# RWKV layer: one-operand feature steps and activation splits move from GpSimd to ScalarE

## The chip, the cores and the metric

The kernel runs on one core of a Trainium2 chip. The metric is the device time of one execution in microseconds (us), as the median of three runs. The engines are named as in the profile: PE is the TensorE matmul and PEld its weight load, DVE is VectorE, ACT is ScalarE, POOL is GpSimd, SP is SyncE, which here issues the DMAs. A name such as L1136 is a line of the kernel before.

## The reference, cut to what matters

The whole program is one gated-recurrence block followed by four layers (convolution, RWKV, attention, convolution) on 512 tokens and 256 context tokens with 1024 channels, in fp32. The change lies in the RWKV layer alone, in what is computed ahead of its recurrence:

```python
xx = centred_shift(h) - h
lerp = lambda n: h + xx * mu[n]
k = lerp(2) @ w_k
v = heads(lerp(3) @ w_v)
kk = heads(k * k_k); kk = kk * rsqrt(sum(kk * kk) + 1e-12)
xw, xa = lerp(1), lerp(4)
for d in range(2):
    w_log = -softplus(-(w0[d] + tanh(xw @ w1[d]) @ w2[d])) - 0.5
    dec = exp(-exp(w_log))
    a = sigmoid(a0[d] + (xa @ a1[d]) @ a2[d])
    dirs.append((heads(dec), heads(k * (1.0 + (a - 1.0) * k_a)), heads(a)))
r = heads(lerp(0) @ w_r)
g = lerp(5) @ w_g
```

The recurrence then runs over these features in both directions, and its output goes through a norm, a gate and a last projection.

## The kernel before

Matrix products keep fp32 precision by a split: an operand becomes a rounded high part (fp32r) and the low part that is left, and three matmuls stand for one product. For weights ScalarE makes the high part (`whi`, L172) and VectorE the low part (`wlo`, L175). For activations `split_x` has a switch: the high part is a copy on GpSimd (L274) or on ScalarE (L272), and the low part a subtraction on VectorE (L275). In the RWKV layer the switch stands at GpSimd everywhere.

The layer has these stages in program order. A matrix `h` of 128 partitions by 8 tiles of 770 columns (tokens and context, channels on partitions) is made. The k projection runs (`proj_fm`, 8 output blocks of 8 k-tiles each), with the low-rank products for decay and `a` fed in between; for its first lerp GpSimd also adds the two neighbours (L1017). The r projection runs next, and after each of its 8 output blocks `features(p)` is called. That makes two units (one for each half of the 768 tokens) of two directions, thus 32 passes of the loop body in `part2`. Then come the g projection (two halves), with the first preparations of the recurrence (`ahead`, whose scores are L1280) placed behind its first half, and the v projection. `part1` makes the two tanh tiles `tz` and `ta` (L1108) from small matmuls (L1105, L1106) in two PSUM banks. For a direction, `part2` then adds 1 to `tz` (L1120, GpSimd), scans it along the tokens (L1123, VectorE), takes two exponentials (L1126, L1127, ScalarE), copies six columns into `pcs` (L1128, GpSimd), and forms the halves of the tiles AR (L1132 VectorE, L1133 GpSimd) and F (L1139 GpSimd, L1141 VectorE) from `kd` (L1136 and L1137, GpSimd) and `ta` (L1140, VectorE, in place, so it waits until L1136 has read `ta`). F and AR go to DRAM by SyncE's queue (L1143) and are read back for the recurrence (L1254). `features` also splits two small weight tiles (`lwh`, L1165, GpSimd).

Each engine carries out its instructions in the order of its own queue. That order is set by a planner that simulates the program with its own costs; weight loads and their splits are given a higher priority. The buffers are few: two of F and AR each, three of `tz`, `ta` and `kd`, eight of `lhi` and `llo` each (the high and low parts of a lerp's eight tiles), two PSUM banks for the small matmuls.

Of the kernel before, what the change touches and what calls it, by code (L numbers as in the profile page):

```python
# [10 lines left out]
F32 = mybir.dt.float32  # L11
F32R = mybir.dt.float32r
AF = mybir.ActivationFunctionType
ALU = mybir.AluOpType
# [4 lines left out]
P = 128  # L19
# [10 lines left out]
FB=[int(c) for c in "2221122333"]  # L30
RB=2
LB=8
BA=[int(c) for c in "0100"]
NE=2
DQ=lambda nc,i: {"s":nc.sync,"a":nc.scalar,"p":nc.gpsimd}["ssss"[i]]
WB=3
# [34 lines left out]
class K:  # L71
# [860 lines left out]
    def rwkv_layer(self, X, XC):  # L932
        nc, ins, tc = self.nc, self.ins, self.tc
# [12 lines left out]
        WH = 770  # L946
# [8 lines left out]
        lp = self.pool(esl, "rwl", side="right")  # L955
        hp = self.pool(esl, "rwh", side="right")
        h = hp.tile([P, KT, WH + 2], F32, name="h")
# [30 lines left out]
        c1 = lp.tile([P, 8], F32, name="c1")  # L988
        c2 = lp.tile([P, 8], F32, name="c2")
        kkc = lp.tile([P, 8], F32, name="kkc")  # L990
        nc.vector.tensor_scalar(w0h, self.col("rwkv_w0_2", 0, 16), 0.5, None, ALU.mult)
        nc.vector.tensor_scalar(a0h, self.col("rwkv_a0_2", 0, 16), 0.5, None, ALU.mult)
        nc.vector.tensor_scalar(c2, self.col("rwkv_k_a_2", 0, 8), 0.5, None, ALU.mult)
# [3 lines left out]
        pcs = lp.tile([P, 2, NP, 12], F32, name="pcs")  # L997
# [9 lines left out]
        def lerp_k(n, k, hi, lo):  # L1007
            t = stg.tile([P, WH], F32, name="l32", bufs=LT)
            nc.vector.scalar_tensor_tensor(t, xx[:, k, :], self.col("rwkv_mu_2", 8 * n + k), h[:, k, 1:WH + 1],
                                           ALU.mult, ALU.add)  # L1010
            self.split_x(hi, lo, t, BA[2] and n in (0, 3, 5))

        def lerped(n, first=False):
            his, los = [], []
            for k in range(KT):
                if first:
                    nc.gpsimd.tensor_tensor(xx[:, k, :], h[:, k, 0:WH], h[:, k, 2:WH + 2], ALU.add)  # L1017
                    nc.vector.scalar_tensor_tensor(xx[:, k, :], xx[:, k, :], 0.5, h[:, k, 1:WH + 1], ALU.mult, ALU.subtract)
                his.append(lerp.tile([P, WH], F32R, name="lhi"))
                los.append(lerp.tile([P, WH], F32R, name="llo"))  # L1020
                lerp_k(n, k, his[k], los[k])
            return (lambda k: his[k]), (lambda k: los[k])
# [43 lines left out]
        def feat(name, i, shape=(P, 384)):  # L1066
            return fp.tile(list(shape), F32, name=name, bufs=FB[i])
# [23 lines left out]
        def part1(p, q, lw):  # L1091

            u = Ctx()
            u.p, u.q, u.n, u.qs = p, q, 2 * p + q, slice(q * 384, (q + 1) * 384)
            u.r, u.k, u.kkh = feat("r", 0), feat("k", 1), feat("kkh", 2)
            nc.sync.dma_start(u.k, k_d[p][:, u.qs])
            for hh in range(2):
                nc.sync.dma_start(u.kkh[hs[hh]], rn_d[2 * p + hh, u.qs].partition_broadcast(64))
            nc.sync.dma_start(u.r, r_d[p][:, u.qs])
            u.tz, u.ta = [], []  # L1100
            for i, x, bias, name, outs in ((0, t1, w0h, "tz", u.tz), (1, a1, a0h, "ta", u.ta)):
                pss = [self.ptr.tile([P, 512], F32, name="tr")[:, :384] for _ in range(2)]
                wh, wl = lw[i]
                for d in range(2):
                    nc.tensor.matmul(pss[d], wh[:, d, :], x[d][:, u.qs], start=True, stop=False)  # L1105
                    nc.tensor.matmul(pss[d], wl[:, d, :], x[d][hs[0], u.qs], start=False, stop=True)  # L1106
                    t = feat(name, 7 + i)
                    nc.scalar.activation(t, pss[d], AF.Tanh, scale=0.5, bias=bias[:, 8 * d + p:8 * d + p + 1])  # L1108
                    outs.append(t)
            return u  # L1110

        def part2(u):
            p, q = u.p, u.q

            nc.vector.scalar_tensor_tensor(u.kkh, u.k, kkc[:, p:p + 1], u.kkh, ALU.mult, ALU.mult)
            u.kds = []
            for d in range(2):

                tz, ta = u.tz[d], u.ta[d]
                (nc.vector if BA[3] == 1 else nc.gpsimd).tensor_scalar(tz, tz, 1.0, 1.0, ALU.mult, ALU.add)  # L1120
                rv = (lambda t: t) if d == 0 else (lambda t: t[:, 383::-1])
                od = (lambda t: t) if d == 0 else (lambda t: t[:, :, 63::-1])
                nc.vector.tensor_tensor_scan(rv(tz), rv(m64[:, d:384 + d]), rv(tz), 0.0, ALU.mult, ALU.add)  # L1123
                Ed = E[(d + 2 * u.n) % len(E)]
                Ein, Eex, en = Ed[:, :, 1 - d:65 - d], Ed[:, :, d:64 + d], 64 * (1 - d)
                nc.scalar.activation(Ein, c3(tz), AF.Exp, scale=-dh)  # L1126
                nc.scalar.activation(tz, tz, AF.Exp, scale=dh)  # L1127
                nc.gpsimd.tensor_scalar(pcs[:, d, p, 6 * q:6 * q + 6].unsqueeze(2), Ed[:, :, en:en + 1], 1.0, 1.0,  # L1128
                                        ALU.mult, ALU.mult)
                F, AR = [feat(nm, i, (P, WH))[:, :TA].rearrange("p (c f t) -> p c f t", f=2, t=64)  # L1130
                         for nm, i in (("F", 5), ("AR", 6))]
                nc.vector.scalar_tensor_tensor(od(AR[:, :, 0, :]), Eex, -2.0, c3(u.kkh), ALU.mult, ALU.mult)  # L1132
                nc.gpsimd.tensor_tensor(AR[:, :, 1, :], Ein, c3(u.r), ALU.mult)  # L1133
                kd = feat("kd", 9)
                (nc.scalar.activation(kd, ta, AF.Identity, scale=c2[:, p:p + 1], bias=c1[:, p:p + 1]) if BA[0]
                 else nc.gpsimd.tensor_scalar(kd, ta, c2[:, p:p + 1], c1[:, p:p + 1], ALU.mult, ALU.add))  # L1136
                (nc.gpsimd if BA[1] else nc.vector).tensor_tensor(kd, kd, u.k, ALU.mult)  # L1137
                u.kds.append(kd)
                nc.gpsimd.tensor_tensor(F[:, :, 1 - d, :], c3(kd), c3(tz), ALU.mult)  # L1139
                nc.vector.scalar_tensor_tensor(ta, ta, 1.0, u.kkh, ALU.add, ALU.mult)  # L1140
                nc.vector.tensor_tensor(od(F[:, :, d, :]), c3(ta), c3(tz), ALU.mult)  # L1141
                for t, dst_ in ((F, f_d[d]), (AR, ar_d[d])):
                    DQ(nc, 1).dma_start(dst_[6 * q:6 * q + 6, :, p].rearrange("c q f t -> q c (f t)"),  # L1143
                                      t.rearrange("q c f t -> q c (f t)"))

            u.bp = u.kds[0]
            nc.vector.tensor_tensor(u.bp, u.kds[0], u.kds[1], ALU.add)
            nc.vector.scalar_tensor_tensor(u.bp, u.r, self.col("rwkv_r_k_2", p), u.bp, ALU.mult, ALU.mult)

        def part3(u):  # L1150
            ps = self.ptr.tile([P, 512], F32, name="tr")
            for i in range(3):
                nc.tensor.matmul(ps[:, 2 * i:2 * i + 2], u.bp[:, i * P:(i + 1) * P], sel2, start=True, stop=True)
            nc.vector.tensor_scalar(bon[:, 3 * u.q:3 * u.q + 3, 2 * u.p:2 * u.p + 2],
                                    ps[:, :6].rearrange("p (i h) -> p i h", h=2), 0.5, None, ALU.mult)

        def features(p):
            lw = []
            for src in (w2, a2):
                wh = fp.tile([P, 2, P], F32R, name="lwh", bufs=2)  # L1160
                wl = fp.tile([64, 2, P], F32R, name="lwl", bufs=2)
                w32 = fp.tile([P, 2, P], F32, name="lw32")
                for hh in range(2):
                    nc.sync.dma_start(w32[hs[hh]], src[:, :, p * P:(p + 1) * P])
                nc.gpsimd.tensor_scalar(wh, w32, 1.0, 1.0, ALU.mult, ALU.mult)  # L1165
                nc.vector.tensor_tensor(wl, w32[hs[0]], wh[hs[0]].bitcast(F32), ALU.subtract)
                lw.append((wh, wl))
            for q in range(2):
                units.append(part1(p, q, lw))
                if len(units) > 2:  # L1170
                    part3(units[-3])
                if len(units) > 1:
                    part2(units[-2])

        def done_r(p, t):
            DQ(nc, 0).dma_start(r_d[p], t)
            features(p)
# [370 lines left out]

        vhi, vlo = [[lerp.tile([P, WH], F32R, name=n) for _ in range(KT)] for n in ("lhi", "llo")]
        for k in range(KT):  # L1550
            self.split_x(vhi[k], vlo[k], h[:, k, 1:WH + 1], BA[2])
        xh, xl = (lambda k: vhi[k]), (lambda k: vlo[k])
        for nh in range(2):
            lnb = bp.tile([P, 512], F32, name="lnb")
# [51 lines left out]
        with ExitStack() as es:  # L1606
            op = self.pool(es, "rwo")
            work = self.pool(es, "rwow", bufs=2)
            hi = op.tile([P, KT, TA], F32R, name="ry_hi")
            lo = op.tile([P, KT, TA], F32R, name="ry_lo")  # L1610
# [427 lines left out]
```

## Time and profile before

| what | value |
|---|---|
| median of 3 runs | 2716.43 us (2715.82 to 2716.82) |
| the profiled execution | 2723.18 us, its span 2721.5 us |
| mean granted TensorE clock over the span | 0.924 |

The busy time of an engine is a share of the whole span; stages differ, so the rows below are of the stretch from 814 us to 1345 us, in which the layer's `h` is finished, the projections and features are made, and the recurrence's first scores begin. A wait is the idle time of an engine ahead of an instruction, put down to what ended it. The granted clock is a share of the full 2.4 GHz, mean over a stretch.

### The profile page before, as it was taken

To read this page: it belongs to the slowest core of one execution; us is meant where nothing else is said; L and a number is where in the kernel's file an instruction comes from. 1 tells how busy PE (TensorE), PEld (TensorE's weight loads), DVE (VectorE), ACT (ScalarE), POOL (GpSimd) and SP (SyncE) were. 2 spreads that over 40 slices of the span, in tenths; PEclk is the share of its full clock that TensorE was granted. 3 is DMA by queue.
4 is the path that set the end of the run, shared out by engine and by line. 5 is a ranking of instruction groups with operands and counts; after the bars stand their busy time and mean duration, and the time that the engine had idled before them with its cause. 6 is when DMAs were issued, how large, how long until landed. Compare 5 with 4: busy or idle time off the path is not lost. (4 is left out here: it accounts for less than half of the span.)

```text
span 2721.5 us, 48392 instructions
## 1 busy us (share of the span) xinstructions
PE 2398.6 (88%) x19837; PEld 1900.8 (70%) x19867; DVE 1693.8 (62%) x2577; ACT 1014.6 (37%) x1861; POOL 714.7 (26%) x700
## 2 busy tenths in 40 slices
PE   6998869899896888898699886889999899997996
PEld 4776657777574766666588775768788788875655
DVE  4434356985457588888678874545255378548836
ACT  4642343111431233232355553233333366422223
POOL 0101001000205269888222541210000178300001
PEclk8998988899897989899599998889999999998998
DMA  5523542434322227655523443533455411222331
GB/s 151 147 85 101 155 140 70 118 90 118 91 85 63 76 93 225 182 183 170 186 96 132 145 141 103 201 106 98 132 155 153 137 43 43 68 93 78 86 95 55
DMA packets 352942, 319.06 MB, mean 117 GB/s; under 512 B 19679, under 2 KB 292032, under 8 KB 352208
## 3 DMA queue, kind: packets, MB, share of 16 engines
q1 hardware_dynamic: 352720, 315.95, 38.4%
q8 instruction: 157, 2.57, 0.4%
q14 instruction: 65, 0.53, 0.1%
HBM read 241.85 MB, written 64.63 MB: 113 GB/s over the span
## 5 line engine op out<-in xcount | busy, mean ns | idle before, releaser
L175 DVE TENSOR_TENSOR wlo<-wraw,whi 128x1024 fp32r<-128x1024 f32 x212 | 268.0, 1265 | 461.9 <-ACT whi L172 446.3
L172 ACT ACTIVATE whi<-wraw 128x1024 fp32r<-128x1024 f32 x212 | 224.2, 1058 | 732.7 <-PE mm L202 414.0
L202 PE MATMUL mm<-hT_lo,whi 128*128 128x512 f32 (+1 forms) x864 | 322.8, 374 | 0.0
L201 PE MATMUL mm<-hT_hi,whi 128*128 128x512 f32 (+1 forms) x864 | 318.4, 380 | 1.0 <-ACT h L680 1.0
L204 PE MATMUL mm<-hT_hi,wlo 128*128 128x512 f32 (+1 forms) x864 | 289.6, 371 | 0.5 <-DVE wlo L175 0.5
L807 DVE SCALAR_TENSOR_TENSOR cvo<-ypad,dwh,cvo 128x784 f32<-128x784 f32 (+1 forms) x270 | 236.4, 905 | 4.5
L204 PEld LDWEIGHTS mm<-hT_hi,wlo 128*128 128x128 f32 x864 | 163.6, 190 | 39.1 <-issue 1.4
L201 PEld LDWEIGHTS mm<-hT_hi,whi 128*128 128x128 f32 x864 | 164.6, 191 | 35.7 <-issue 13.0
L202 PEld LDWEIGHTS mm<-hT_lo,whi 128*128 128x128 f32 x864 | 164.6, 191 | 33.0 <-issue 6.3
L220 PE MATMUL mm<-whi,hT_hi 128*128 128x512 f32 x384 | 152.7, 399 | 1.3 <-ACT hT_hi L265 1.3
L221 PE MATMUL mm<-wlo,hT_hi 128*128 128x512 f32 x384 | 152.6, 397 | 0.0
L222 PE MATMUL mm<-whi,hT_lo 128*128 128x512 f32 x384 | 149.8, 399 | 0.0
L767 POOL MEMSET ypad<- 128x15 f32 x16 | 1.8, 114 | 500.2 <-DVE cvo L807 274.0
L201 PE MATMUL mm<-lhi,whi 128*128 128x256 f32 (+1 forms) x256 | 83.5, 369 | 16.8 <-POOL lhi L274 15.6
L202 PE MATMUL mm<-llo,whi 128*128 128x256 f32 (+1 forms) x256 | 89.3, 370 | 8.7 <-DVE llo L275 8.5
L220 PE MATMUL mm<-whi,lhi 128*128 128x512 f32 x192 | 82.7, 433 | 11.3 <-DVE so L1536 5.9
L220 PEld LDWEIGHTS mm<-whi,hT_hi 128*128 128x128 f32 x384 | 72.7, 189 | 19.0 <-issue 2.4
L221 PE MATMUL mm<-wlo,lhi 128*128 128x512 f32 x192 | 80.9, 421 | 5.7 <-DVE wlo L175 5.7
L585 PE MATMUL tr<-mraw,sc 128*32 128x128 f32 x1536 | 68.2, 295 | 18.1 <-DMA mraw<-in_mod_w_dram 14.0
L221 PEld LDWEIGHTS mm<-wlo,hT_hi 128*128 128x128 f32 x384 | 72.6, 189 | 15.6 <-issue 1.2
L222 PEld LDWEIGHTS mm<-whi,hT_lo 128*128 128x128 f32 x384 | 71.9, 189 | 15.9 <-issue 1.8
L1287 ACT ACTIVATE Df<-ps 32x128 f32<-32x128 f32 x176 | 68.1, 387 | 37.5 <-PE ps L1280 35.2
(502 smaller groups left out, 5897.0 us busy)
## 6 DMA issues: line engine op xcount, KB each, us to landing
mraw<-in_mod_w_dram SPq DMA_DIRECT2D x96, 512.0 KB
wraw<-in_conv_w_in_dram SPq DMA_DIRECT2D x48, 512.0 KB
wraw<-in_attn_w_in_dram SPq DMA_DIRECT2D x48, 512.0 KB
wraw<-in_w_in_dram SPq DMA_DIRECT2D x24, 512.0 KB
f_d<-F SPq DMA_DIRECT2D x32, 384.0 KB
ar_d<-AR SPq DMA_DIRECT2D x32, 384.0 KB
F<-f_d SPq DMA_DIRECT2D x24, 512.0 KB
AR<-ar_d SPq DMA_DIRECT2D x24, 512.0 KB
```

The costliest lines, as they stand in the source:

```text
L172: nc.scalar.activation(hi[:, :n], raw, AF.Copy)
L175: nc.vector.tensor_tensor(lo[:, :n], raw, hi[:, :n].bitcast(F32), ALU.subtract)
L201: nc.tensor.matmul(ps[s], wh[:, k, :], xh(k)[:, a:b], start=k == 0, stop=False)
L202: nc.tensor.matmul(ps[s], wh[:, k, :], xl(k)[:, a:b], start=False, stop=False)
L204: nc.tensor.matmul(ps[s], wl[:, k, :], xh(k)[:, a:b], start=False, stop=k == kts - 1)
L220: nc.tensor.matmul(ps, h, wh[:, kk, :], start=k == 0, stop=False)
L221: nc.tensor.matmul(ps, h, wl[:, kk, :], start=False, stop=False)
L222: nc.tensor.matmul(ps, l, wh[:, kk, :], start=False, stop=k == kts - 1)
L585: nc.tensor.matmul(ps[g:g + 32, 0:P], self.sc[:, k, :], raw[:, k, :], start=k < 4, stop=k >= 4)
L767: nc.gpsimd.memset(yp_[:, 0:15], 0.0)
L807: nc.vector.scalar_tensor_tensor(acc, yp_[:, tap:tap + W], dwh[:, tap, kt:kt + 1], acc, ALU.mult, ALU.add)
L1287: nc.scalar.activation(s.Df[rows, :, :, gsl].rearrange("p t a u -> p u a t"), p3[rows, :, 32 * b:32 * b + 32].rearrange("p u (a t) -> p u ...
```

## The change

Five steps move from GpSimd to ScalarE; what is computed stays the same. The activation splits of all lerps (of 770 columns: 24 into `lhi` and 16 low-rank ones into F) and of the 8 tiles for v make their high part on ScalarE. In `part2`, `tz + 1` becomes an activation with a bias operand (a new tile `one`, set once), `pcs` a copy, and `kd`'s first step an activation with a scale and a bias operand. In `features` the copy into `lwh` moves. The split of the squares in `done_k` (L1076) stays on GpSimd, as do the products with two tensor operands (L1133, L1137, L1139). The line of L1137 is only rewritten: it ran on GpSimd before as well.

```diff
+        one = lp.tile([P, 1], F32, name="one")
+        nc.vector.memset(one, 1.0)
...
-            self.split_x(hi, lo, t, BA[2] and n in (0, 3, 5))
+            self.split_x(hi, lo, t, True)
...
-                (nc.vector if BA[3] == 1 else nc.gpsimd).tensor_scalar(tz, tz, 1.0, 1.0, ALU.mult, ALU.add)
+                nc.scalar.activation(tz, tz, AF.Identity, bias=one)
...
-                nc.gpsimd.tensor_scalar(pcs[:, d, p, 6 * q:6 * q + 6].unsqueeze(2), Ed[:, :, en:en + 1], 1.0, 1.0,
-                                        ALU.mult, ALU.mult)
+                nc.scalar.activation(pcs[:, d, p, 6 * q:6 * q + 6].unsqueeze(2), Ed[:, :, en:en + 1], AF.Copy)
...
-                (nc.scalar.activation(kd, ta, AF.Identity, scale=c2[:, p:p + 1], bias=c1[:, p:p + 1]) if BA[0]
-                 else nc.gpsimd.tensor_scalar(kd, ta, c2[:, p:p + 1], c1[:, p:p + 1], ALU.mult, ALU.add))
-                (nc.gpsimd if BA[1] else nc.vector).tensor_tensor(kd, kd, u.k, ALU.mult)
+                nc.scalar.activation(kd, ta, AF.Identity, scale=c2[:, p:p + 1], bias=c1[:, p:p + 1])
+                nc.gpsimd.tensor_tensor(kd, kd, u.k, ALU.mult)
...
-                nc.gpsimd.tensor_scalar(wh, w32, 1.0, 1.0, ALU.mult, ALU.mult)
+                nc.scalar.activation(wh, w32, AF.Copy)
...
-            self.split_x(vhi[k], vlo[k], h[:, k, 1:WH + 1], BA[2])
+            self.split_x(vhi[k], vlo[k], h[:, k, 1:WH + 1], True)
```

## Rows read from the trace of the kernel before

**Rows 1.** The page, busy time of each engine over the span.

```profile
PE 2398.6 (88%) x19837; PEld 1900.8 (70%) x19867; DVE 1693.8 (62%) x2577; ACT 1014.6 (37%) x1861; POOL 714.7 (26%) x700
```

**Rows 2.** Stretches: us, busy us of PE, PEld, DVE, ACT, POOL; clock; DMA.

```profile
814.00:860.00 46.00, 21.86 (x78) 15.47 (x78) 38.76 (x32) 11.04 (x20) 30.07 (x23) 0.65 0.21 70
...
968.00:1120.00 152.00, 131.32 (x570) 98.47 (x568) 133.18 (x132) 46.18 (x87) 134.56 (x104) 0.90 0.52 159
1120.00:1200.00 80.00, 69.76 (x269) 50.06 (x269) 71.60 (x83) 28.32 (x51) 69.77 (x64) 0.94 0.64 197
1200.00:1295.00 95.00, 81.70 (x325) 60.61 (x323) 79.36 (x104) 29.09 (x52) 75.87 (x70) 0.91 0.59 183
1295.00:1345.00 50.00, 31.68 (x255) 27.51 (x256) 33.64 (x83) 17.37 (x41) 13.56 (x15) 0.55 0.61 199
```

**Rows 3.** PE's waits, 814 to 1295 us: total, times, longest.

```profile
PE mm L201 <- POOL lhi L274: 15.6, 3, 11.5
...
PE tr L1105 <- ACT ta L1108: 4.0, 3, 1.4
```

**Rows 4.** POOL's groups by line and shape, 815 to 1310 us.

```profile
L1136 POOL TENSOR_SCALAR kd<-ta,c,c 128x384 f32<-128x384 f32 x32 | 48.1, 1503 | 2.3 <-ACT ta L1108 1.3 <-POOL pcs L1128 0.9
L1133 POOL TENSOR_TENSOR AR<-E,r 128x384 f32<-128x384 f32 x32 | 45.6, 1427 | 12.7 <-DMA r<-r_d 12.7
...
L274 POOL TENSOR_SCALAR lhi<-l 128x770 fp32r<-128x770 f32 x24 | 35.4, 1478 | 7.6 <-DVE l L1009 6.6 <-DVE bon L1154 0.9
L1120 POOL TENSOR_SCALAR tz<-tz 128x384 f32<-128x384 f32 x32 | 31.8, 1000 | 1.0 <-ACT tz L1108 1.0
L1128 POOL TENSOR_SCALAR pcs<-E 128x6 f32<-128x6 f32 x32 | 20.1, 629 | 16.3 <-ACT E L1126 14.8 <-DMA kkh<-rn_d 1.5
...
L274 POOL TENSOR_SCALAR F<-l 128x770 fp32r<-128x770 f32 x16 | 15.8, 985 | 24.2 <-PE tr L1078 14.5 <-DVE l L1009 6.6 <-DVE t L1051 2.0
```

**Rows 5.** DVE's groups by line and shape, 815 to 1310 us.

```profile
L1123 DVE TENSOR_TENSOR_SCAN tz<-m,tz 128x384 f32<-128x384 f32 x32 | 38.3, 1208 | 2.6 <-POOL tz L1120 2.5
L1141 DVE TENSOR_TENSOR F<-ta,tz 128x384 f32<-128x384 f32 x32 | 32.9, 1028 | 1.3 <-ACT tz L1127 0.7
L1140 DVE SCALAR_TENSOR_TENSOR ta<-ta,kkh 128x384 f32<-128x384 f32 x32 | 27.9, 870 | 19.0 <-POOL kd L1136 19.0
```

**Rows 6.** Single lines: shortest, median and longest instruction in ns.

```profile
L1120 POOL TENSOR_SCALAR tz<-tz x32: 507/815/4348, 968.8 to 1275.3; 128x384 f32<-128x384 f32 x32
...
L1123 DVE TENSOR_TENSOR_SCAN tz<-m,tz x32: 920/956/1767, 976.6 to 1276.6; 128x384 f32<-128x384 f32 x32
...
L1141 DVE TENSOR_TENSOR F<-ta,tz x32: 541/1246/1641, 988.4 to 1287.3; 128x384 f32<-128x384 f32 x32
...
L1140 DVE SCALAR_TENSOR_TENSOR ta<-ta,kkh x32: 539/633/1645, 985.0 to 1286.0; 128x384 f32<-128x384 f32 x32
```

**Rows 7.** DVE's waits, 968 to 1295 us: total, times, longest.

```profile
DVE ta L1140 <- POOL kd L1136: 19.0, 21, 3.3
DVE lwl L1166 <- POOL lwh L1165: 5.2, 4, 2.5
```

**Rows 8.** ACT's waits, 968 to 1295 us: total, times, longest.

```profile
ACT E L1126 <- DVE tz L1123: 101.9, 25, 8.3
```

**Rows 9.** ACT's groups by line and shape, 815 to 1310 us.

```profile
L1108 ACT ACTIVATE tz<-tr,w0h 128x384 f32<-128x384 f32 x32 | 18.2, 580 | 41.7 <-DVE F L1141 22.3 <-PE tr L1106 10.5 <-POOL F L1139 5.4
...
L964 ACT ACTIVATE h<-mm,mod,gs 128x512 f32<-128x512 f32 x8 | 5.8, 797 | 0.0
...
L1050 ACT ACTIVATE t<-F 64x768 fp32r<-64x768 f32 x2 | 1.7, 843 | 0.2 <-POOL F L1048 0.2
L1108 ACT ACT_TABLE_LOAD x1 | 1.3, 1283 | 0.0
```

**Rows 10.** Timeline, SyncE: a late store of F, the first reading back.

```profile
1289.75 0.39 SPq L1143 DMA_DIRECT2D f_d<-F  x1
...
1294.18 0.44 SPq L1254 DMA_DIRECT2D F<-f_d  x1
```

More of the change, by code (lines that the diff above doesn't have):

```diff
@@ L32 @@
 LB=8
-BA=[int(c) for c in "0100"]
 NE=2
```

## Prediction

> **What bounds the kernel now.** I read the page first. PE is the busiest engine, POOL the least busy one [rows 1], so over the whole span nothing seems to be won by taking work from POOL. The share over the span misleads here: the table of stretches shows that POOL's work is bunched. From 968 to 1120 us POOL is busy 134.56 of 152 us (89%), DVE 133.18 (88%), PE 131.32 (86%) and ACT 46.18 (30%); the next two stretches look alike [rows 2]. Over these three, 327 us, ACT's share is 103.6 us (46.18 + 28.32 + 29.09), or 32%. Three engines are near full, each waits for the others, and the fourth has room.
>
> Which of the three sets the pace? I looked at waits next. PE's recorded waits for POOL's `lhi` are 15.6 us in three pieces, one of them 11.5 us, and those are all at the starts of projections [rows 3]. In the body of the features the wait that stands out is ACT's: 25 times, 101.9 us in all, an exponential waits for DVE's scan [rows 8]. ACT is thus not short of time, it is behind DVE. DVE in turn idles 19.0 us, 21 times, until L1136 on POOL has read `ta`, and 5.2 us until POOL has made `lwh` [rows 7]. And while DVE is busy, it is slow: L1141 takes 541 ns at its shortest and 1246 ns at the median, and POOL's L1120 goes from 507 ns to 4348 ns [rows 6]. Instructions of one shape that vary so much are held up by something else that runs; I read it as DVE and POOL getting in each other's way. So the pace of the features is DVE's, stretched and interrupted by POOL.
>
> The end of the stage counts too. A late F store is issued at 1289.75 us, the first reading back at 1294.18 us [rows 10], and from 1295 to 1345 us PE runs at a mean granted clock of 0.55 with 31.68 of 50 us busy [rows 2]: the scores have nothing to hide under, because features and projections end together. Features that end sooner than the projections would change that.
>
> **The change part by part.** I count on the profiled execution's own time, 2723.2 us (span 2721.5 and 1.7 around it); that is 6.8 us above the median of 2716.4, and the difference that I find is taken off the median.
>
> *What POOL loses.* L1136 48.1 us, L1120 31.8, L1128 20.1, the 24 `lhi` splits 35.4, the 16 F splits 15.8: 151.2 us [rows 4], and besides these 16 small `lwh` copies and the last 8 `lhi` splits, which I leave out of the sum. No DMA moves: the stores of F and AR stay in SyncE's queue and come when the features are done.
>
> *What ACT gains.* `tz + 1` is like the tanh of the same shape, 32 x 0.58 = 18.6 us; `kd` lies between that and the 512-column activation with scale and bias operands (0.797), I take 0.69, 32 x 0.69 = 22.1; `pcs` lies between nothing and 0.58, for six columns I take 0.3, 9.6; `lwh` at most 0.58, I take 0.5, 16 x 0.5 = 8.0; a split as the copy of 768 columns, 0.843 [rows 9], and 24 of them fall into the 327 us, 20.2. Together 78.5 us, so ACT goes from 103.6 to 182 us of 327 (56%). Some 24 more splits, 20.2 us, fall before 968 us, where ACT has 35 of 46 us free in the first stretch [rows 2].
>
> *814 to 860 us.* POOL gives up eight splits behind its eight neighbour sums, and PE's wait of 11.5 us is for one of these splits [rows 3]. DVE is busy 38.76 of 46 us here [rows 2] and makes three operations per tile itself, so it takes over as the limit soon. Bounds: nothing to 11.5 us. I take 5.
>
> *860 to 968 us.* The 16 low-rank F splits leave a POOL that is not full (15.8 us in 16 pieces, mean 985 ns, [rows 4]) for an ACT that has one of 843 ns [rows 9]. I take nothing; what hides it is the k projection's matmul stream. If a split there sticks behind a weight split that waits for a buffer, it costs some microseconds; that is in the bounds.
>
> *968 to 1295 us, DVE's waits.* `kd` now follows the tanh in ACT's own queue, so `ta` is read well before DVE comes to overwrite it: the 19.0 us go, and with `lwh` the 5.2: 24 us [rows 7].
>
> *968 to 1295 us, DVE's stretching.* The excess over the shortest is 32 x (1208 - 920) = 9.2 us for the scan, 32 x (1028 - 541) = 15.6 for L1141, 32 x (870 - 539) = 10.6 for L1140 [rows 5, 6]; 35.4 us for the three. How much goes with the moved operations? L1136, L1120 and L1128 make 100.0 us [rows 4] of POOL's 280.2 us (134.56 + 69.77 + 75.87) [rows 2], 36%. I take that share, 13 us. Bounds: nothing (the kept products fill the place) and 35.
>
> A rule of the Trainium skill speaks against this part (GPSIMD Engine Reference, section 4.1, Engine selection): it calls one-input operations on GpSimd roughly line rate and two-input ones about twice slower, so the change takes away what that engine does well and leaves what it does badly. The shortest L1120, 507 ns against 580 ns for the tanh of this shape on ACT [rows 6, 9], agrees. If that were all, the sum would be no gain at all, against my 13 and 24 us; it feeds the third rival.
>
> *What ACT's fuller queue costs.* The queue is in order. Behind an exponential that waits for the scan now stand more things that others need: `whi` splits, PSUM evictions, `lhi`. PE waited 4.0 us for ACT's `ta` [rows 3]. With ACT's work up by three quarters (182 over 103.6) I take 7 us as the price. Bounds: 3 and, worked out below, 66.
>
> *The sum.* -5 - 24 - 13 + 7 = -35 us. DVE is busy nearly nine tenths of the time, so I let it through to the end in full. PE could follow: over the 327 us it is busy 282.8 (131.32 + 69.76 + 81.70), at a clock of 0.90 to 0.94 [rows 2], so with fewer gaps and a fuller clock it needs well under 290. That gives 2688 us by the profiled execution, and 2716.4 - 35 = about 2681 us as the median.
>
> **The rivals.**
>
> *First, the recurrence's first scores slip under the projections.* If the planner lets the features end clearly before the v projection, the 50 us from 1295 to 1345 us, at clock 0.55 [rows 2], are partly covered by matmuls of v. For it: features are held by DVE and POOL, and both get lighter. Against: PE's queue spreads the small matmuls of the features evenly along g and v, and both end together now [rows 10]. If half of the 50 us is hidden, 2681 - 25 = 2656 us; if nearly all, 2635.
>
> *Second, slower: splits stuck in ACT's queue.* The mechanism is one: an `lhi` split for the r or g projection stands behind an exponential that waits for the scan, on average 101.9 / 25 = 4.1 us, at most 8.3 [rows 8], and PE, which cannot go on without that tile, stops, as it did when POOL was late [rows 3]. There are 16 such splits. All of them stuck cost 16 x 4.1 = 66 us: 2681 + 66 - 7 = 2740 us. It decides when the cost, instead of 7, reaches 42 + 5, that is with 12 stuck splits. For it: ACT's wait is frequent in just this stretch. Against: if DVE gets faster, that wait gets shorter, and the planner puts the splits of later tiles ahead.
>
> *Third, no change.* The kept products with two operands stand between the same neighbours (L1133 alone 45.6 us, two more like it, [rows 4]), and hold DVE up as long as before; the waits of rows 7 become waits for L1137, which still follows `kd` on POOL. Then only the first 5 us and ACT's 7 us stay: about 2716 us.
>
> *Fourth, table loads.* A load of ACT's function table takes 1283 ns, and one was seen at L1108 [rows 9]. No row shows this kind of bias activation between tanh and exponential. If each of the 64 moved ones brought a pair of loads, that would be 64 x 2 x 1.283 = 164 us, 2881 us. One load for 64 tanh says that tanh, copies and exponentials already share a table, so a small chance remains for the scaled form. The Trainium skill (ScalarE: Activation LUTs, Table sets: the hidden batching unit) says that cheap functions, identity and copy among them, are in every set; by that rule the chance would be nil.
>
> **How the numbers follow.** The forecast 0.52, first rival 0.16, second 0.20, third 0.10, fourth 0.02. A measurement here can tell about 0.2%, 5.4 us, from no change. The forecast's own range is 2660 to 2708 us: upper end with no gain in the stretching and in the first stretch and a cost of ACT of 15 (-24 + 15 = -9), lower end with all 35 of the stretching gone (-5 - 24 - 35 + 7 = -57). The whole range, 2632 to 2730 us, takes in the first rival down to nearly all hidden and the second up to about 14 stuck splits (14 x 4.1 - 42 = 15); it leaves out the rest of the second (0.10), a little beyond the first (0.03) and the fourth (0.02). Faster: forecast and first rival, 0.68. Same: 0.10. Slower: second and fourth, 0.22.
>
> **What would show it.** Right: in the new profile DVE's wait for `kd` at L1140 is nearly gone, L1141's median falls below 1.0 us, POOL is busy near half of the 327 us, ACT near 55%, and the last F store comes 30 us earlier. The first rival shows as scores among matmuls of v. The second shows as PE waits for `lhi` on ACT of several microseconds, with an exponential's wait ahead of them. The third shows as DVE times of the same medians. The prediction is wrong if PE, though its suppliers are faster, meets new waits in its planned order.

## The result and the profile after

The median goes from 2716.12 to 2673.08 us. The ratio is 0.9842, with a 95% interval of 0.9823 to 0.9861: 43 us, or 1.6%, faster. The forecast was 2681 us.

The page of the changed kernel, busy time of each engine over its span of 2670.6 us, answers to [rows 1]:

```profile
PE 2379.7 (89%) x19837; PEld 1890.7 (71%) x19867; DVE 1653.5 (62%) x2578; ACT 1095.9 (41%) x2021; POOL 581.7 (22%) x540
```

POOL is 133 us less busy and ACT 81 us more, with 160 instructions moved from the one to the other. DVE, which got one instruction more (the memset), is 40 us less busy.

The same stages in the table of stretches (columns as in [rows 2]; the stage borders lie earlier now):

```profile
810.00:857.00 47.00, 26.91 (x99) 20.58 (x99) 36.78 (x36) 20.66 (x32) 26.64 (x13) 0.64 0.31 98
...
958.00:1107.00 149.00, 134.63 (x606) 102.33 (x605) 129.01 (x150) 86.09 (x168) 89.14 (x47) 0.94 0.59 179
1107.00:1180.00 73.00, 71.50 (x285) 52.39 (x284) 62.44 (x82) 44.47 (x87) 37.38 (x29) 0.95 0.77 235
1180.00:1251.00 71.00, 63.86 (x267) 46.63 (x265) 63.12 (x86) 32.57 (x66) 46.99 (x32) 0.98 0.61 186
1251.00:1295.00 44.00, 25.31 (x163) 22.01 (x165) 30.71 (x68) 15.31 (x36) 14.30 (x15) 0.53 0.68 221
```

The features' stretch, the middle three rows, takes 293 us where it took 327. ACT is busy 163.1 of it (56%), POOL 173.5 (59%), DVE 254.6 (87%). PE is busy 270.0 us (92%, where it was 86%) and runs at a clock of 0.94 to 0.98. The last row is as thin as it was: the scores still stand bare.

VectorE's waits from 958 to 1251 us, which answer to [rows 7]:

```profile
DVE kd L1146 <- POOL kd L1136: 11.9, 4, 5.2
DVE kd L1147 <- DMA r<-r_d: 9.1, 1, 9.1
...
DVE lwl L1165 <- ACT lwh L1164: 2.2, 1, 2.2
DVE ta L1139 <- ACT kd L1135: 2.1, 1, 2.1
```

The 21 waits for kd at the line that overwrites `ta` (now L1139) shrank from 19.0 to 2.1 us, that for `lwh` from 5.2 to 2.2. But new ones are there: 11.9 us for the product kd times k (now L1136), which still runs on GpSimd, and 9.1 us, once, for a load of r.

VectorE's lines in the changed kernel, from 811 to 1266 us, and shortest, median and longest of two of them; they answer to [rows 5, 6]:

```profile
L1124 DVE TENSOR_TENSOR_SCAN tz<-m,tz 128x384 f32<-128x384 f32 x32 | 30.8, 968 | 3.1 <-ACT tz L1121 3.1
L1139 DVE SCALAR_TENSOR_TENSOR ta<-ta,kkh 128x384 f32<-128x384 f32 x32 | 29.7, 929 | 2.1 <-ACT kd L1135 2.1
L1140 DVE TENSOR_TENSOR F<-ta,tz 128x384 f32<-128x384 f32 x32 | 28.0, 875 | 1.3 <-ACT tz L1128 0.7
```

```profile
L1140 DVE TENSOR_TENSOR F<-ta,tz x32: 527/560/1528, 981.8 to 1242.9; 128x384 f32<-128x384 f32 x32
...
L1139 DVE SCALAR_TENSOR_TENSOR ta<-ta,kkh x32: 522/790/1574, 976.7 to 1241.9; 128x384 f32<-128x384 f32 x32
```

The scan is nearly undisturbed (mean 968 instead of 1208 ns). The F product's median fell from 1246 to 560 ns, but `ta`'s mean rose from 870 to 929. ScalarE's wait for the scan went from 101.9 to 45.9 us, and a new one came up, its splits waiting for the lerp:

```profile
ACT E L1127 <- DVE tz L1124: 45.9, 23, 5.1
ACT lhi L271 <- DVE l L1010: 17.3, 6, 7.7
```

The moved steps on ScalarE, from 811 to 1266 us, and the one table load at the tanh:

```profile
L1135 ACT ACTIVATE kd<-ta,c,c 128x384 f32<-128x384 f32 x32 | 22.5, 702 | 3.0 <-PE tr L1152 2.5 <-DVE kd L1146 0.2
L271 ACT ACTIVATE lhi<-l 128x770 fp32r<-128x770 f32 x24 | 20.1, 843 | 30.2 <-DVE l L1010 30.2
L1121 ACT ACTIVATE tz<-tz,one 128x384 f32<-128x384 f32 x32 | 19.4, 612 | 0.4
...
L1164 ACT ACTIVATE lwh<-lw 128x256 fp32r<-128x256 f32 x16 | 6.6, 411 | 16.0 <-DMA lw<-in_rwkv_a_dram 14.6 <-PE tr L1106 1.2 <-DMA lw<-in_rwkv_w_dram 0.2
L1129 ACT ACTIVATE pcs<-E 128x6 f32<-128x6 f32 x32 | 6.3, 198 | 0.0
...
L1109 ACT ACT_TABLE_LOAD x1 | 1.3, 1283 | 0.0
```

TensorE's waits from 810 to 1251 us, which answer to [rows 3], show what the fuller queue of ScalarE costs:

```profile
PE tr L1079 <- POOL F L273: 11.8, 3, 5.5
...
PE mm L200 <- ACT lhi L271: 8.3, 4, 4.0
PE tr L1152 <- ACT ta L1109: 3.9, 1, 3.9
```

SyncE's last store of F and the first reading back, which answer to [rows 10]:

```profile
1245.02 0.36 SPq L1142 DMA_DIRECT2D f_d<-F  x1
...
1248.64 0.45 SPq L1253 DMA_DIRECT2D F<-f_d  x1
```

The last store comes 44.7 us earlier, and the reading back still follows it at once.

### The profile page after: what moved, and what is told of

Its sections match the earlier page's. It is cut to its first block, busy times and chain, and to the rows that moved or that the text cites. A ratio compares the mean times of both kernels' runs of the same rounds, so it can differ in the third digit from the quotient of the medians.

```text
span 2670.6 us, 48383 instructions
## 1 busy us (share of the span) xinstructions
PE 2379.7 (89%) x19837; PEld 1890.7 (71%) x19867; DVE 1653.5 (62%) x2578; ACT 1095.9 (41%) x2021; POOL 581.7 (22%) x540
## 5 line engine op out<-in xcount | busy, mean ns | idle before, releaser
L201 PE MATMUL mm<-llo,whi 128*128 128x512 f32 (+1 forms) x256 | 88.9, 368 | 10.5 <-DVE llo L274 10.5
L200 PE MATMUL mm<-lhi,whi 128*128 128x512 f32 (+1 forms) x256 | 84.4, 368 | 8.9 <-ACT lhi L271 8.3
L219 PEld LDWEIGHTS mm<-whi,hT_hi 128*128 128x128 f32 x384 | 72.7, 189 | 18.7 <-issue 2.2
L584 PE MATMUL tr<-mraw,sc 128*32 128x128 f32 x1536 | 67.1, 292 | 17.4 <-DMA mraw<-in_mod_w_dram 14.5
L1136 POOL TENSOR_TENSOR kd<-kd,k 128x384 f32<-128x384 f32 x32 | 71.6, 2237 | 47.9 <-ACT kd L1135 35.2
```

The source lines that it names most:

```text
L200: nc.tensor.matmul(ps[s], wh[:, k, :], xh(k)[:, a:b], start=k == 0, stop=False)
L201: nc.tensor.matmul(ps[s], wh[:, k, :], xl(k)[:, a:b], start=False, stop=False)
L219: nc.tensor.matmul(ps, h, wh[:, kk, :], start=k == 0, stop=False)
L584: nc.tensor.matmul(ps[g:g + 32, 0:P], self.sc[:, k, :], raw[:, k, :], start=k < 4, stop=k >= 4)
L1136: nc.gpsimd.tensor_tensor(kd, kd, u.k, ALU.mult)
```

## The experiments

Each was timed in five rounds against the kernel before, on the same chip as it, on one of three occasions; the kernel before took 2711.9 us (e1 to e4), 2716.0 (e5 to e8) and 2713.2 (e9 to e12) there. The changed kernel was not timed again beside them, so a comparison with it goes by the ratios. The gain in us is worked out from the ratio on the 2716 us of before.

| run | on ScalarE, or what else differs | ratio (95%) | gain, us |
|---|---|---|---|
| the change | all | 0.9842 (0.9823 to 0.9861) | 43 |
| e1_features | tz, pcs, kd, lwh | 0.9924 (0.9912 to 0.9936) | 21 |
| e2_splits | all splits | 0.9933 (0.9921 to 0.9946) | 18 |
| e3_pool_reads | all, and reads added on GpSimd | 0.9909 (0.9895 to 0.9923) | 25 |
| e4_pool_writes | all, and memsets added on GpSimd | 0.9878 (0.9865 to 0.9892) | 33 |
| e5_kd | kd | 0.9924 (0.9910 to 0.9938) | 21 |
| e6_no_kd | all but kd | 0.9871 (0.9849 to 0.9893) | 35 |
| e7_squares | all, and the squares' splits | 0.9841 (0.9822 to 0.9861) | 43 |
| e8_late_splits | splits for r, g, v | 0.9917 (0.9901 to 0.9933) | 23 |
| e9_kd_late | kd and splits for r, g, v | 0.9919 (0.9905 to 0.9932) | 22 |
| e10_small_steps | tz, pcs, lwh | 0.9940 (0.9928 to 0.9952) | 16 |
| e11_kdmul_vector | all, and kd times k on VectorE | 0.9844 (0.9819 to 0.9869) | 42 |
| e12_f_vector | all, and kd times tz on VectorE | 0.9821 (0.9807 to 0.9834) | 49 |

### The two halves

e1_features, the changed kernel with the splits back on GpSimd:

```diff
-            self.split_x(hi, lo, t, True)
+            self.split_x(hi, lo, t)
...
-            self.split_x(vhi[k], vlo[k], h[:, k, 1:WH + 1], True)
+            self.split_x(vhi[k], vlo[k], h[:, k, 1:WH + 1])
```

> The changed kernel with all activation splits back on GpSimd; tz + 1, pcs, kd and lwh stay on ScalarE. My theory (the pace of the features is VectorE's, held up by GpSimd's one-operand steps; of the sum, 24 + 13 us are theirs and 5 the splits'): most of the 43 us stays, 2682 us (2677 to 2690). Rival (the gain comes from the starts of the projections, where TensorE waited for GpSimd's splits): 2700 us or more.

It takes 2691.89 us, a little beyond my range and half of the gain. e2_splits is the other half:

```diff
-                nc.scalar.activation(tz, tz, AF.Identity, bias=one)
+                nc.gpsimd.tensor_scalar(tz, tz, 1.0, 1.0, ALU.mult, ALU.add)
...
-                nc.scalar.activation(kd, ta, AF.Identity, scale=c2[:, p:p + 1], bias=c1[:, p:p + 1])
+                nc.gpsimd.tensor_scalar(kd, ta, c2[:, p:p + 1], c1[:, p:p + 1], ALU.mult, ALU.add)
...
-                nc.scalar.activation(wh, w32, AF.Copy)
+                nc.gpsimd.tensor_scalar(wh, w32, 1.0, 1.0, ALU.mult, ALU.mult)
```

(`pcs` in the same way.)

> The other half: only the activation splits on ScalarE, the feature steps back on GpSimd. My theory: some 5 us of gain, 2706 to 2712 us. Rival (starts of the projections): 2690 us or less. If both halves gain much less than together 43 us, they help each other: GpSimd gets free only with both.

It takes 2694.67 us, 11 us less than my expectation's fast end. The halves add up to 39 of the 43 us, but the splits weigh nearly as much as the feature steps. The sum had given them 5 us.

### Where the splits' gain sits

e8_late_splits is e2_splits with the condition that the early lerps stay on GpSimd:

```diff
-            self.split_x(hi, lo, t, True)
+            self.split_x(hi, lo, t, n in (0, 5))
```

> The kernel before with only the late splits on ScalarE: the lerps of the r and g projections and the tiles of v, which fall among the features; the early ones (k and the low-rank products) stay on GpSimd, and so do all feature steps. All splits together gained 18 us. If that comes from the start of the k projection: this one gains under 6 us, 2706 or more where before takes 2712. If it comes from GpSimd having 44 us less to do among the features, whatever step it is: a gain of 10 to 15, 2697 to 2702 us.

The late splits alone gain 23 us, at least as much as all of them and more than the 10 to 15 that I had expected. So the gain of the splits is not at the start of the k projection; it comes among the features. The 5 us that I gave the first stretch can't be seen in the times at all.

### One step of the features, and the rest

e5_kd is the kernel before with kd's scaled form alone moved:

```diff
-                (nc.scalar.activation(kd, ta, AF.Identity, scale=c2[:, p:p + 1], bias=c1[:, p:p + 1]) if BA[0]
-                 else nc.gpsimd.tensor_scalar(kd, ta, c2[:, p:p + 1], c1[:, p:p + 1], ALU.mult, ALU.add))
+                nc.scalar.activation(kd, ta, AF.Identity, scale=c2[:, p:p + 1], bias=c1[:, p:p + 1])
```

> The kernel before with one step moved: kd's scaled form (one activation in each of the 32 passes) on ScalarE, all else on GpSimd as before. The prediction gives the wait of VectorE for this step 19 us. If that wait lay on the path: 2690 to 2697 us where before takes 2712. If what counts is GpSimd's total work (kd is 48 of the 172 us of it that the change takes off GpSimd, thus 28%, and the change as a whole gains 43): 12 us, 2700 us. If waits are only handed on to L1137, which still runs on GpSimd: 2708 us or more.

It gains 21 us, within the case of a wait on the path (15 to 22 us). Its complement e6_no_kd, the changed kernel with

```diff
-                nc.scalar.activation(kd, ta, AF.Identity, scale=c2[:, p:p + 1], bias=c1[:, p:p + 1])
+                nc.gpsimd.tensor_scalar(kd, ta, c2[:, p:p + 1], c1[:, p:p + 1], ALU.mult, ALU.add)
```

> The complement: the changed kernel with only kd's scaled form back on GpSimd. Wait on the path: it loses 15 to 22 of the 43 us, 2685 to 2692 us on the scale where before takes 2712 and the changed kernel 2669. GpSimd's total work: it loses 12, 2681 us. Waits handed on: within 4 us of the changed kernel.

loses only 8 us of the 43, at 2680.91 us. That is less than a wait on the path would cost, and it lies between the other two cases, 12 us and 4; with some 8 us of uncertainty to either side these two are not told apart. The trace says why it is so little: with kd back on GpSimd VectorE waits 13.4 us for it again, but the wait of 11.9 us for the product kd times k shrinks to 0.9. So the same step is worth 21 us when it goes first and 8 when it goes last. e10_small_steps moves `tz`, `pcs` and `lwh` alone (their three lines of the change, the rest as before):

> The rest of the feature steps alone: tz + 1, pcs and lwh on ScalarE; kd and all splits on GpSimd. They take 65 us of GpSimd's busy time off. If kd and the late splits are the whole change: nothing, within 5 us of before. If it is GpSimd's work that counts: 10 to 18 us faster, 2696 to 2704 where before takes 2714. If the scan was held up by its hop to GpSimd: the same gain, with ScalarE's wait for the scan shorter.

It gains 16 us, as the theory of GpSimd's work says, and against the one that kd and the late splits are everything. The third case, the hop, expects the same gain and is not told apart by the time. ScalarE's wait for the scan is indeed shorter here (77.2 us instead of 101.9), but so it is in e8_late_splits (73.4), where the hop stays; and VectorE's own wait for `tz + 1` from GpSimd was only 2.5 us before. e9_kd_late tried just kd and the late splits:

> Two parts alone: kd's scaled form and the late splits (lerps of r and g, tiles of v) on ScalarE; tz + 1, pcs, lwh and the early splits stay on GpSimd. Each of the two alone gained 21 to 23 us. If they are the whole change: together about 43 us, as the changed kernel, 2671 us where before takes 2714. If a gain is set by how much work GpSimd has left: these take 92 of 172 us off, thus 20 to 30 us, 2684 to 2694.

22 us, no more than either of them alone, and within the second case. The parts overlap: what they have in common is that GpSimd has less to do among the features, and each of the three groups of steps gains 16 to 23 us when it goes first.

The table of stretches shows where the time goes. For each kernel the stretch from the first scan to the last F product (columns as in [rows 2]); first the kernel before, then the change, then e5_kd, e8_late_splits, e9_kd_late and e12_f_vector, each from its own trace:

```profile
976.60:1287.90 311.30, 271.97 (x1110) 200.76 (x1109) 269.36 (x304) 99.73 (x183) 269.90 (x232) 0.91 0.58 178
```

```profile
967.70:1244.10 276.40, 254.99 (x1080) 189.28 (x1079) 240.03 (x300) 157.44 (x311) 165.76 (x104) 0.95 0.66 200
```

```profile
974.30:1267.50 293.20, 256.62 (x1084) 189.30 (x1083) 265.17 (x301) 119.60 (x212) 236.68 (x199) 0.95 0.61 188
```

```profile
971.50:1267.00 295.50, 265.06 (x1106) 194.79 (x1105) 251.92 (x303) 116.14 (x202) 249.57 (x211) 0.93 0.62 188
```

```profile
970.40:1256.90 286.50, 263.70 (x1126) 194.53 (x1125) 252.42 (x303) 135.61 (x236) 211.19 (x180) 0.96 0.64 193
```

```profile
966.80:1235.10 268.30, 250.46 (x1079) 187.39 (x1078) 236.03 (x331) 158.76 (x310) 130.49 (x70) 0.96 0.67 206
```

The stretch gets shorter from 311.3 to 268.3 us, and VectorE's share of it stays near where it was: 87%, 87%, 90%, 85%, 88%, 88%. POOL's share goes from 87% to 49%.

What VectorE loses differs. In e5_kd it is mostly idle time, 41.9 us before and 28.0 now, while its busy time hardly falls (269.4 to 265.2). In e8_late_splits it is busy time alone: 269.4 to 251.9 us with 43.6 us idle, and its wait for kd is still 18.7 us. So GpSimd held VectorE up in two ways, by results that came late and by making VectorE's own instructions longer, and each of these two parts takes mainly one of them away. The whole change takes 29.3 us of busy time and 5.6 us of idle time out of the stretch.

This fits a pace that VectorE sets, but does not settle it. TensorE's share goes from 87% to 92% in the change and 93% in e12_f_vector; in the changed kernel it is idle for 21.4 us of the stretch, less than VectorE's 36.4. No run tells which of the two would hold the stretch next. The granted clock does not order the runs: it is 0.95 in e5_kd with 293.2 us and 0.95 in the change with 276.4.

### GpSimd's reading or GpSimd's queue

e3_pool_reads adds work on GpSimd that nobody waits for, ahead of the product that reads `u.k` there anyway:

```diff
+                scr = fp.tile([P, 256], mybir.dt.bfloat16, name="scr")
+                for _ in range(3):
+                    nc.gpsimd.tensor_scalar(scr, u.k[:, :256], 1.0, 1.0, ALU.mult, ALU.mult)
                 nc.gpsimd.tensor_tensor(kd, kd, u.k, ALU.mult)
```

> The changed kernel with three more GpSimd instructions in each of the 32 passes, which read 256 columns of k into a scratch tile that nobody reads; they stand ahead of the product that reads k on GpSimd anyway, so no other engine waits for them. If GpSimd's reading itself holds VectorE up: VectorE's two-operand steps get longer again and the time rises by 10 to 20 us, to 2683 to 2693 us. If only the waits for GpSimd's results counted (kd, lwh): 2673 us, within 4.

e4_pool_writes puts memsets there:

```diff
+                scr = fp.tile([P, 256], mybir.dt.bfloat16, name="scr")
+                nc.gpsimd.tensor_scalar(scr[:, :6], u.k[:, :6], 1.0, 1.0, ALU.mult, ALU.mult)
+                for _ in range(4):
+                    nc.gpsimd.memset(scr, 0.0)
                 nc.gpsimd.tensor_tensor(kd, kd, u.k, ALU.mult)
```

> The same place, but with four memsets of the scratch tile (and one read of 6 columns that ties them to the place) instead of the three reads: GpSimd is about as busy and reads next to nothing. If reading is what holds VectorE up: under 2678 us, and VectorE's steps as short as in the changed kernel. If it is GpSimd's fuller queue that makes its products late: the same rise as with the reads.

The reads lose 18 of the 43 us, as expected in size; the memsets lose 10, which neither side had said. VectorE's busy time, which was to rise with the reads, did not. The stretch from first scan to last F product and the longest of VectorE's waits in it, for the reads and then for the memsets:

```profile
965.50:1260.60 295.10, 262.25 (x1078) 193.39 (x1077) 239.82 (x300) 157.62 (x310) 240.52 (x188) 0.93 0.62 188
...
DVE kd L1149 <- POOL kd L1139: 22.0, 7, 7.9
```

```profile
967.00:1251.40 284.40, 257.72 (x1074) 190.14 (x1073) 236.08 (x300) 157.12 (x310) 221.59 (x244) 0.94 0.64 195
...
DVE kd L1150 <- POOL kd L1140: 16.9, 6, 5.3
```

VectorE is busy 239.8 and 236.1 us, no more than the 240.0 of the change. It waits longer instead: its idle time in the stretch is 55.3 and 48.3 us against 36.4, and of that 22.0 and 16.9 us are for kd times k, against 11.9 in the change. These 18.9 and 11.9 us more of idle time are about what the two runs lose. A GpSimd that is filled up again delays its own products, and VectorE waits for those. Single lines of VectorE do change with the reads, one for the worse and one for the better (shortest, median and longest; the medians were 560 and 790 ns in the change):

```profile
L1143 DVE TENSOR_TENSOR F<-ta,tz x32: 537/1024/1534, 979.6 to 1259.4; 128x384 f32<-128x384 f32 x32
...
L1142 DVE SCALAR_TENSOR_TENSOR ta<-ta,kkh x32: 521/620/1370, 974.5 to 1258.4; 128x384 f32<-128x384 f32 x32
```

Reads cost more than memsets, but GpSimd is also busier with them (240.5 against 221.6 us), so the reading itself is not told apart from the queue. Nor are the added reads the steps that the change took away: they write 256 columns of 16 bits, those 384 or 770 columns of 32 bits.

### The kept products

e11_kdmul_vector moves the product that VectorE now waits for:

```diff
-                nc.gpsimd.tensor_tensor(kd, kd, u.k, ALU.mult)
+                nc.vector.tensor_tensor(kd, kd, u.k, ALU.mult)
```

> The changed kernel with one of the three kept products, kd times k, on VectorE. VectorE gets 32 instructions of 0.55 us, 17.6 us, and loses its wait of 11.9 us for this product and the 15 us by which its own instructions run long beside it. If the kept products are what still holds VectorE up: no loss or up to 10 us gained, 2661 to 2671 where the changed kernel takes 2671. If VectorE's own work sets the pace: 10 to 18 us slower.

e12_f_vector moves another one and leaves the first on GpSimd:

```diff
-                nc.gpsimd.tensor_tensor(F[:, :, 1 - d, :], c3(kd), c3(tz), ALU.mult)
+                nc.vector.tensor_tensor(F[:, :, 1 - d, :], c3(kd), c3(tz), ALU.mult)
```

> The same with the other product, kd times tz into F, on VectorE: 17.6 us of work more, some 24 us of stretching beside it gone. Kept products as the hold-up: no loss or up to 8 us gained. VectorE's own work as the pace: 10 to 18 us slower, 2681 to 2689 where the changed kernel takes 2671.

2671.55 and 2664.38 us: no loss that is clear of the noise, and the second is the fastest kernel of the study. Its interval (0.9807 to 0.9834) overlaps that of the change, so that it beats the change is likely and not settled. VectorE's lines in e12_f_vector, from 965 to 1236 us:

```profile
L1140 DVE TENSOR_TENSOR F<-ta,tz 128x384 f32<-128x384 f32 x32 | 23.3, 728 | 0.6 <-DMA f_d<-F 0.3
L1139 DVE SCALAR_TENSOR_TENSOR ta<-ta,kkh 128x384 f32<-128x384 f32 x32 | 23.1, 723 | 1.4 <-ACT kd L1135 1.4
L1138 DVE TENSOR_TENSOR F<-kd,tz 128x384 f32<-128x384 f32 x31 | 23.0, 741 | 5.8 <-POOL kd L1136 5.8
```

VectorE has taken over 23.0 us of products, and its busy time over the stretch went from 240.0 to 236.0. The two other lines alone got 28.0 - 23.3 + 29.7 - 23.1 = 11.3 us shorter. In e11_kdmul_vector, over the same window, it is 28.0 - 22.6 + 29.7 - 19.8 = 15.3 us:

```profile
L1140 DVE TENSOR_TENSOR F<-ta,tz 128x384 f32<-128x384 f32 x32 | 22.6, 710 | 0.8 <-ACT tz L1128 0.7
L1136 DVE TENSOR_TENSOR kd<-kd,k 128x384 f32<-128x384 f32 x32 | 20.9, 654 | 3.2 <-ACT kd L1135 3.0
L1139 DVE SCALAR_TENSOR_TENSOR ta<-ta,kkh 128x384 f32<-128x384 f32 x32 | 19.8, 619 | 0.0
```

Here the two engines getting in each other's way is shown for GpSimd's products with two tensor operands. That its one-operand steps do it too is suggested by e8_late_splits: only such steps leave GpSimd there, and VectorE's busy time in the stretch falls by 17.4 us.

### A remaining wait

e7_squares moves the split of the squares and of the low-rank results as well:

```diff
-            self.split_x(hi, lo, sq)
+            self.split_x(hi, lo, sq, True)
...
-                nc.gpsimd.tensor_scalar(hi, t, 1.0, 1.0, ALU.mult, ALU.mult)
+                nc.scalar.activation(hi, t, AF.Copy)
```

> The changed kernel with two more steps on ScalarE: the high part of the squares in the k projection (8 of 768 columns) and of the low-rank results (2). TensorE still waits 11.8 us for the split of squares there in the changed kernel, always for GpSimd behind ScalarE's square. If the hop between engines is what costs: 4 to 8 us faster than the changed kernel, 2661 to 2665 on the scale where before takes 2712. If the wait is for the square itself, which sits behind a weight split in ScalarE's queue: no change, 2669 within 3.

Nothing gained. TensorE's wait there from 857 to 958 us was 8.1 us for POOL in the change and is now, in e7_squares,

```profile
PE tr L1079 <- ACT F L271: 8.4, 2, 6.0
```

so the wait is for the square and not for the hop. In the change ScalarE is never idle ahead of one of the 8 squares (L1076): the square comes late out of its queue.

## Why the prediction was right, and where it was not

*The pace is VectorE's, held up by GpSimd: the second half shown, the first argued.* e3_pool_reads and e4_pool_writes put work on GpSimd and on no other engine and lose 18 and 10 us; taking work off it gains with whatever step goes first. That VectorE and not TensorE sets the pace fits the stretches above and is not shown by them.

*VectorE's waits, 24 us: right in kind, mostly given back.* 19.0 + 5.2 us became 2.1 + 2.2. But 11.9 us of wait for kd times k and 9.1 us for a load of r came up, which the sum did not have, though it named the first in the third rival. VectorE's idle time in the stretch fell by 5.6 us only.

*VectorE's stretching, 13 us: near for the three lines, too small as a whole.* By the same formula the excess is now 32 x (968 - 921) + 32 x (875 - 527) + 32 x (929 - 522) ns = 1.5 + 11.1 + 13.0 = 25.6 us (921 ns is the scan's shortest here), 9.8 less than the 35.4. But VectorE's whole busy time between first scan and last F product fell by 269.36 - 240.03 = 29.3 us. The step that was mis-sized is here: I let only L1136, L1120 and L1128 count as work taken from GpSimd among the features and only three lines as relieved, and left the late `lhi` splits out. In e8_late_splits these alone take 17.4 us off VectorE's busy time and gain 23 us.

*The sum: in part luck.* The two terms came to 24 + 13 = 37 us and measured 5.6 + 29.3 = 34.9, because the first was 18 us too large and the second 16 too small.

*That one-operand steps hold VectorE up by reading: open.* Reads put back (e3_pool_reads) left VectorE's busy time as it was and made its waits longer; the splits taken away (e8_late_splits) made it less busy. That the kept products stretch VectorE is shown by e11_kdmul_vector and e12_f_vector.

*The first stretch, 5 us: in the traces, not in the times.* All splits gain no more than the late ones. But until 960 us TensorE's waits for the first lerps' high and low parts are 11.5 + 7.7 us before and 5.7 + 9.3 in the change, 4.2 us less. The first scan starts between 962.9 and 968.0 us in the eight traces with the early splits on ScalarE, and between 970.4 and 976.6 in the six others.

*ScalarE's load, 78.5 us: right; its price, 7 us: near what the waits show.* Measured are 22.5 for kd, 19.4 for tz, 6.3 for pcs, 6.6 for lwh and 24 x 0.843 = 20.2 for the late splits, 75.0 together. TensorE's waits for ScalarE's `lhi` (8.3 us) and `ta` (3.9) are 8.2 us more than the 4.0 of before, and are what the second rival described, four pieces and one piece instead of twelve. What they cost in time was not tested.

*The rivals.* The first did not come: the stretch behind the features is as thin as before (clock 0.53), though it begins 45 us earlier. The third (whose time by its own terms is 2716.4 - 5 + 7 = 2718 us) falls with the stretching, though half of its wait came, the 11.9 us for kd times k; the fourth falls with the single table load at L1109. The rule of the Trainium skill that I had weighed against the change (GPSIMD Engine Reference, section 4.1, Engine selection) is borne out by e12_f_vector in one half, that two-operand work is what GpSimd is bad at: kd times tz took 1295 ns on GpSimd in the change and 741 on VectorE. Its other half, that one-operand work is fit for it, did not decide here: taking that away from a GpSimd that was 87% busy among the features gained 43 us.

*Open.* The parts do not add up in a simple way: kd and the late splits gain 21 and 23 us apart and 22 together, while in their traces the features' stretch is 18.1, 15.8 and 24.8 us shorter than before. Of the 50.9 us by which the changed kernel's profiled span is shorter, 34.9 lie in that stretch, 8.9 ahead of it and 7.1 behind it. The profiled execution of the kernel before was itself 7 us above its median, so a few us of any difference between profiles can be that execution's. Each build is also planned anew, and a kernel that only changes the planner's order was not run; how much of the 16 to 23 us of every single part is the old order's bad luck is therefore not settled.

## What to carry to other kernels

Look at the engine that is least busy over the span in the stretch where it works: an engine at 26% overall can be nearly full for 300 us and hold its neighbour up. When a queue like that is taken apart, each piece alone may gain as much as two together, so time the pieces in more than one order before judging what one is worth. Part of a slow engine's time can come from the engine beside it, so split what a change gains into busy time and idle time before naming a cause. If VectorE runs long beside GpSimd's two-operand products, try those on VectorE itself: here 32 of them came at no cost.

## What was not expected of the hardware

32 products of two tensors moved from GpSimd to VectorE raised VectorE's own work by 23.0 us and lowered its busy time from 240.0 to 236.0 us. And 96 extra reads on GpSimd, which raised its busy time in the stretch by 75 us (165.8 to 240.5), left VectorE's busy time where it was (240.0 and 239.8) and lengthened its waits.
